# One kernel, one change: the weight panels of merge and output projection are split by ScalarE and VectorE instead of GpSimd

## The chip, the core and the metric

The kernel runs on one core of a Trainium2 chip. A core has five engines, each with its own queue of instructions, taken in order: TensorE (matrix products, into PSUM), VectorE and ScalarE (elementwise work, from and to SBUF and PSUM), GpSimd (elementwise work, SBUF only) and SyncE, which here issues all the DMA transfers. Engines wait for one another by semaphores. The metric is the time of one execution on the device, in microseconds.

In the profile's rows PE is TensorE (PEld its loads of stationary operands), DVE is VectorE, ACT is ScalarE, POOL is GpSimd and SP is SyncE; a q behind a name means the engine's sequencer.

## The reference, cut to what matters

One layer of a hybrid encoder is computed for two requests of 512 and 1024 tokens, 1536 tokens of 1024 channels in all. After the attention branch (`att`) and the state space branch (`y_ssm`) come:

```python
g = jax.nn.sigmoid(gates.reshape(b, S, 2, D_MODEL))
merged = g[:, :, 0] * (att @ w_proj_attn) + g[:, :, 1] * (y_ssm @ w_proj_ssm)
m = merged @ w_out
x = x + rmsnorm(m, norm_post_mix[l])
h = rmsnorm(x, norm_pre_ffn[l])
gate, up = jnp.split(h @ w_gate_up[l], 2, axis=-1)
f = (jax.nn.silu(gate) * up) @ w_down[l]
x = x + rmsnorm(f, norm_post_ffn[l])
```

All of it is float32. `w_proj_attn` and `w_out` are 1024 x 1024.

## The kernel before

**Products.** Every product is made of three: each operand `raw` is split into a high part `hi`, `raw` rounded to the matmul's reduced type, and a low part `lo = raw - hi`. `gemm` (L161) then adds hi x hi, hi x lo and lo x hi in PSUM, which are its lines L164, L165 and L166. So each weight panel costs a cast and a subtraction. `split` (L133) makes them, and its argument says on which engines: "act_dve" casts on ScalarE (L135) and subtracts on VectorE (L136), "act_pool" casts on ScalarE and subtracts on GpSimd (L138, L139), anything else does both on GpSimd (L141, L142).

**Panels.** `split_panel` (L144) loads a panel of 1024 x 256 weights in two halves of 128 partitions x 1024 elements, each of 512 KB, into tiles `wraw` (pool `rp`, two buffers), and splits each half into `whi` and `wlo` (pool `wp`, two buffers each, so two panels). By default it splits with "act_dve".

**The stages around the change.** The tokens go through the last part of the kernel in three chunks of 512. For chunk c:

- `load_att(c)` (L347): per head, loads a piece of attention and a broadcast row of scales (`araw`, three buffers), multiplies them (L353, VectorE), splits the product by "act_dve".
- `merge(c)` (L882): four panels of `w_proj_attn`, two blocks of 128 channels each. Per block: load `gt` (two buffers) and `pt` (one buffer), tanh of `gt` (L893, ScalarE), 24 matmuls of 512 columns, then L897 (VectorE, one input in PSUM), L898 (VectorE), L899 (ScalarE, high part of the result) and L900 (VectorE, its low part).
- `out_proj` (L1027): four panels of `w_out`, per panel four PSUM tiles of 24 matmuls of 256 columns each, each evicted by two ScalarE operations (L1035, L1037).
- `norms(c)` (L1040): two normalisations of the result. On VectorE L1053 and L1054 in eight pieces of 512 columns, each with a load of x (`xr`, two buffers) and a square on ScalarE (L1055), a chain of very small VectorE operations (`rsqrt`, L178 to L183), four L1061, then transposes on TensorE (L1065), evicted by ScalarE (L1067) and stored.

Chunk 0 has been merged during attention. The program writes, in this order: `out_proj` of chunk 0, `merge(1)`, `norms(0)`, `load_att(2)`, `out_proj` of chunk 1, `merge(2)`, `norms(1)`, the operands of the feed-forward's first product (`Operands`, `build`, VectorE and ScalarE), `out_proj` of chunk 2, first products, `norms(2)`.

**Order.** The order in which each engine takes its instructions is not the program's: a planner (`schedule_with_timeline_sim=True`) orders them by simulated times and its own costs, within the dependencies and the buffers. So work of one stage stands between that of another, and other engines for a piece of work can mean another order elsewhere. All loads and stores go through SyncE's one queue in the planned order: an issue that waits for a buffer holds those behind it.

Of the kernel before, what the change touches and what calls it, by code (L numbers as in the profile page):

```python
# [78 lines left out]
def hybrid_trunk_kernel(ctx: ExitStack, tc: tile.TileContext, a: dict, y_prompt, y_sample):  # L79
# [5 lines left out]
    def f(ap):  # L85
        return ap.bitcast(F32)
# [40 lines left out]
    def staged(pool, shape, *srcs, tag="raw", bufs=None):  # L127
        raw = pool.tile(shape, F32, tag=tag, name=tag, bufs=bufs)
        for part, src in srcs:
            load(out=raw[part] if part is not None else raw, in_=src)  # L130
        return raw

    def split(hi, lo, raw, eng=None):  # L133
        if eng == "act_dve":
            S.copy(hi, raw)  # L135
            V.tensor_sub(lo, raw, f(hi))  # L136
        elif eng == "act_pool":
            S.copy(hi, raw)  # L138
            G.tensor_sub(lo, raw, f(hi))  # L139
        else:  # L140
            G.tensor_scalar(hi, raw, 1.0, 0.0, op0=ALU.mult, op1=ALU.add)  # L141
            G.tensor_sub(lo, raw, f(hi))  # L142

    def split_panel(*srcs, eng="act_dve"):  # L144
        hi = wp.tile([P, KB, 256], F32R, tag="whi", name="whi")
        lo = wp.tile([P, KB, 256], F32R, tag="wlo", name="wlo")
        n = 256 // len(srcs)
        for s in (slice(0, 4), slice(4, 8)):
            raw = rp.tile([P, 4, 256], F32, tag="wraw", name="wraw")
            for i, src in enumerate(srcs):  # L150
                load(out=raw[:, :, i * n:(i + 1) * n], in_=src.rearrange("(a p) c -> p a c", p=P)[:, s])
            split(hi[:, s], lo[:, s], raw[:], eng)
        return hi, lo
# [20 lines left out]
        gemm(ps, [(act[0][:, k, ts_], act[1][:, k, ts_], hi[:, k, :], lo[:, k, :]) for k in range(KB)])  # L174

    def rsqrt(r, v, t):
        """r = v ** -0.5 for positive v: a first guess from the exponent, then Newton's steps"""
        V.tensor_scalar(r.bitcast(I32), v.bitcast(I32), 1, None, op0=ALU.logical_shift_right)  # L178
        V.tensor_scalar(r.bitcast(I32), r.bitcast(I32), -1.0, 1597463007.0, op0=ALU.mult, op1=ALU.add)
        for _ in range(3):  # L180
            V.tensor_mul(t, r, r)
            V.scalar_tensor_tensor(t, t, -0.5, v, op0=ALU.mult, op1=ALU.mult)
            V.scalar_tensor_tensor(r, t, 1.5, r, op0=ALU.add, op1=ALU.mult)  # L183
# [29 lines left out]
                next(others, None)  # L213

    def operands(base, SL, h, qk, qr, got):
        """the bias table, queries and keys of a head, in steps"""
        nkb = SL // P
        u0, un = P * (8 - nkb), SL + P * (nkb - 1)
        tb = qk.tile([P, un], F32, tag="tb", name="tb")
        load(out=tb, in_=sk_d[h, :, 127 + u0:127 + u0 + un])  # L220
        got["tb"] = tb
        halves = [slice(o, o + 512) for o in range(0, SL, 512)]
        for m in range(2):
            r = slice(h * P + m * 64, h * P + m * 64 + 64)
            q_h = qk.tile([P, SL], F32R, tag=f"qh{m}", name="qh")
            q_l = qk.tile([P, SL], F32R, tag=f"ql{m}", name="ql")
            q_r = staged(qr, [P, SL], *((slice(o, o + 64), q_d[r, base:base + SL]) for o in (0, 64)))
            S.copy(q_h[:], q_r[:])  # L228
            for s_ in halves:
                with behind():  # L230
                    G.tensor_sub(q_l[:, s_], q_r[:, s_], f(q_h[:, s_]))  # L231
                if QS: yield
            yield
            k_m = qk.tile([P, SL], F32R, tag=f"km{m}", name="km")
            k_r = staged(qr, [P, SL], *((slice(o, o + 64), k_d[r, base:base + SL]) for o in (0, 64)))
            S.copy(k_m[:], k_r)
            for s_ in halves:
                with behind():
                    G.tensor_sub(k_m[64:P, s_], k_r[64:P, s_], f(k_m[64:P, s_]))
                if QS: yield  # L240
            got[m] = (q_h, q_l, k_m)
            yield
# [3 lines left out]
    def behind():  # L246
        return tc.issue_after(last_add[-1].ins) if last_add and IA else nullcontext()
# [81 lines left out]
            pend.append(mean_square)  # L329

    def att_scale(g, zq, msq, pool, psp, ptag):
        """what the rows of attention are multiplied by: 1 / sum of exponentials and the norm"""
        n = zq.shape[-1]
        r, t = [pool.tile([P, 8, n], F32, tag=t_, name=t_, bufs=1) for t_ in ("att_r", "att_t")]
        V.reciprocal(t, zq)
        V.tensor_mul(zq, msq, t)
        V.tensor_mul(zq, zq, t)
        V.tensor_scalar(zq, zq, 1.0, EPS, op0=ALU.mult, op1=ALU.add)
        rsqrt(r[:], zq[:], msq[:])
        V.tensor_mul(r, r, t)  # L340
        ps = psp.tile([P, 512], F32, tag=ptag, name="rt")
        TE.transpose(ps[0:8 * n, 0:P], r[:].rearrange("p h j -> p (h j)"), ident)
        rt = pool.tile([P, P], F32, tag="att_rt", name="rt", bufs=1)
        V.tensor_copy(rt[0:8 * n], ps[0:8 * n, 0:P])
        store(out=r_d[g][:], in_=rt[0:8 * n])
# [10 lines left out]

    w_in = a["w_in"][0]

# [1 line left out]
    with ExitStack() as ph1:  # L360
        hp = ph1.enter_context(tc.tile_pool(name="hp", bufs=NCH, reuse_waits="tile"))
        st = ph1.enter_context(tc.tile_pool(name="st", bufs=2, reuse_waits="tile"))
# [4 lines left out]
        with tc.tile_pool(name="xa", bufs=2, reuse_waits="tile") as xa, tc.tile_pool(name="xa_ps", bufs=3, space=PSUM) as xps:  # L367
            natural_log_exp()
            for c in range(NCH):
# [19 lines left out]
                for j, xt in enumerate(tiles):  # L389
# [3 lines left out]
                    r = rsqrt_of(xa, ss, 1.0 / D, f"rs{j}")  # L393
# [49 lines left out]
        first = [split_panel(w_in[:, V0 + p0:V0 + p0 + 256], eng="pool") for p0 in (0, 256)]  # L443
# [57 lines left out]
        att_scale(0, zq, msq, pools[1], pools[5], "t")  # L501
        es.close()

        # step sizes and decays, for both directions at once
        sp = ph1.enter_context(tc.tile_pool(name="sp", bufs=1, reuse_waits="tile"))
        dts = sp.tile([P, NT, 32], F32, name="dts")
        tri = sp.tile([P, 2, P], F32, name="tri")
# [162 lines left out]
        for lo_c, hi_c in SEQS:  # L670
            state = [None, None]
# [40 lines left out]
        for lo_c, hi_c in SEQS:  # L712
            state = [None, None]
# [67 lines left out]

        gates(NG, 2 * D // P)

# [1 line left out]
    ap = ctx.enter_context(tc.tile_pool(name="ap", bufs=1, reuse_waits="tile"))  # L785
    zq, msq = [ap.tile([P, 8, 8], F32, name=n) for n in ("zq", "msq")]
    with ExitStack() as ph2:
# [3 lines left out]
        at = ph2.enter_context(tc.tile_pool(name="at", bufs=2, reuse_waits="tile"))  # L791
# [63 lines left out]
            pass  # L855
        pend.pop()()

# [1 line left out]
    with ExitStack() as ph3:  # L859
        big = ph3.enter_context(tc.tile_pool(name="big", bufs=7, reuse_waits="tile"))  # L860
        wk = ph3.enter_context(tc.tile_pool(name="wk", bufs=2, reuse_waits="tile"))
# [20 lines left out]
        def merge(c, aTt):  # L882
            cs = slice(c * 512, (c + 1) * 512)
            hi, lo = big_pair()
            for p0 in range(0, D, 256):
                w = split_panel(a["w_proj_attn"][0][:, p0:p0 + 256], eng="pool")
                for b in range(2):
                    r0 = p0 + b * P
                    kb = r0 // P
                    gt = wk.tile([P, 512], F32, tag="gt", name="gt")  # L890
                    pt = wk.tile([P, 512], F32, tag="pt", name="pt", bufs=1)
                    load(out=gt, in_=g_d[r0:r0 + P, cs])
                    S.activation(out=gt, in_=gt, func=AF.Tanh, scale=0.5)  # L893
                    load(out=pt, in_=part_d[r0:r0 + P, cs])
                    ps = mm_tile(512)
                    gemm_fm(ps, w, slice(b * P, (b + 1) * P), aTt)
                    V.scalar_tensor_tensor(gt, gt, 1.0, ps, op0=ALU.add, op1=ALU.mult)  # L897
                    V.tensor_add(gt, gt, pt)  # L898
                    S.activation(out=hi[:, kb, :], in_=gt, func=AF.Copy, scale=0.5)  # L899
                    V.scalar_tensor_tensor(lo[:, kb, :], gt, 0.5, f(hi[:, kb, :]), op0=ALU.mult, op1=ALU.subtract)  # L900
            return hi, lo

        # the feed-forward's first product by Strassen's scheme in Winograd's form: seven products of half size
        class Operands:
            names = ("b11", "t2", "t3", "t1", "b21", "t4", "b22")
            terms = {"b11": [(0, 0)], "t2": [(1, 1), (0, 1), (0, 0)], "t3": [(1, 1), (0, 1)], "t1": [(0, 1), (0, 0)],
# [115 lines left out]
        with ExitStack() as ph3a:  # L1022
# [4 lines left out]
            def out_proj(mT):  # L1027
                tiles = [mp.tile([P, D], F32, tag="mt", name="mt", bufs=4) for _ in range(4)]
                sums = wk.tile([P, 4, 4], F32, tag="ms4", name="ms4")
                for p0 in range(0, D, 256):  # L1030
                    w = split_panel(a["w_out"][0][:, p0:p0 + 256], eng="pool")
                    for j in range(4):
                        ps = mm_tile(256)
                        gemm_tm(ps, w, mT, slice(j * P, (j + 1) * P))
                        S.copy(tiles[j][:, p0:p0 + 256], ps)  # L1035
                        sq = wk.tile([P, 256], F32, tag="gt", name="msq")
                        S.activation(out=sq, in_=ps, func=AF.Square, accum_out=sums[:, j, p0 // 256:p0 // 256 + 1])  # L1037
                return tiles, sums
# [52 lines left out]
            w = {jb: weights(jb, "pt", 1) for jb in range(NPRE + NW)}  # L1091
# [17 lines left out]
    with ExitStack() as ph4:  # L1109
# [9 lines left out]
        for hf in range(2):  # L1119
# [11 lines left out]
            for t in range(NT):  # L1131
# [22 lines left out]
                r = rsqrt_of(yp, ss, 1.0 / D, "rs")  # L1154
# [44 lines left out]
```

## Time and profile before

| | us |
|---|---|
| three runs | 3272.72, 3287.25, 3288.95 |
| their median | 3287.25 |
| span of the profiled execution, first to last instruction | 3277.1 |

The profiled execution is one of its own; its time beside its span is not given apart, so only the span is known of it. It lies 10.2 us below the median of the runs.

A profile's page gives each engine's busy time, the span in 40 slices, the costliest groups of instructions by line, and the chain of work that ended last, followed back from the last instruction. Line numbers are the kernel's. In rows with arrows the tile that is written stands left of "<-". A helper's line, such as L142, stands for all its callers, and the tiles' names tell them apart.

### The profile page before, as it was taken

The page shows a single profiled execution, that of the slowest core. Times are in us where ns is not written, and L with a number is a line of the kernel's source. Part 1 is how long each engine was busy: PE and PEld are TensorE (multiplying, and loading weights), DVE is VectorE, ACT ScalarE, POOL GpSimd, SP SyncE. Part 2 cuts the span into 40 slices and gives each one's busy share as a digit, 9 for nine tenths or more (in the row PEclk, how much of TensorE's full clock was granted, in tenths as well). Part 3 has the DMA queues.
Part 4 walks back from the last instruction along what each step waited for, and adds up shares of the span by engine and source line. Part 5 has one row for each costly group of instructions (what it writes and reads, how often), then busy time and mean ns, then how long its engine had stood idle before and what let it go on. Part 6 is the DMA issues. An engine that isn't in the chain of part 4 may idle for free.

```text
span 3277.1 us, 44930 instructions
## 1 busy us (share of the span) xinstructions
PE 3068.7 (94%) x16688; PEld 2686.3 (82%) x16688; DVE 1887.9 (58%) x3048; ACT 1207.8 (37%) x2249; POOL 1086.4 (33%) x844
## 2 busy tenths in 40 slices
PE   7999999999899899999999888878999899989998
PEld 7988887889787677778888787677999899978787
DVE  5124444455238998277778765676656766642444
ACT  3013333233113333266666623243333333332343
POOL 1003332000244553167657544533333433310100
PEclk9999999999999999999999998888999999999999
DMA  4623332223553443655545146544333333363354
GB/s 145 193 97 114 112 100 76 67 74 108 174 164 124 130 133 118 200 168 172 178 144 182 39 139 221 172 132 154 98 97 106 96 100 99 110 202 94 117 166 131
DMA packets 442528, 430.00 MB, mean 131 GB/s; under 512 B 25324, under 2 KB 359617, under 8 KB 441245
## 3 DMA queue, kind: packets, MB, share of 16 engines
q1 hardware_dynamic: 442309, 427.12, 41.8%
q8 instruction: 132, 2.16, 0.3%
q14 instruction: 87, 0.71, 0.1%
HBM read 315.37 MB, written 120.05 MB: 133 GB/s over the span
## 4 chain that ended last, share of the span: by engine, by line
PE 57%; DVE 14%; DMA 12%; issue 8%; POOL 5%; ACT 4%; SPq 1%; POOLq 0%; DVEq 0%; ACTq 0%
PE acc L164 8%; PE acc L165 8%; PE acc L166 8%; PE mm L164 4%; PE mm L165 4%; PE mm L166 4%; PE d L166 3%; PE d L164 3%; PE d L165 3%; DMA wraw<-in_w_gate_up_dram 2%; DVE m L758 2%; DMA raw<-k_d 2%; DMA araw<-r_d 1%; PE s L290 1%; DVE m L752 1%
## 5 line engine op out<-in xcount | busy, mean ns | idle before, releaser
L164 PE MATMUL acc<-hT,whi 128*128 128x512 f32 (+1 forms) x1080 | 433.6, 402 | 5.8 <-ACT st L434 5.6
L165 PE MATMUL acc<-hT,whi 128*128 128x512 f32 (+1 forms) x1080 | 431.4, 399 | 0.0
L166 PE MATMUL acc<-hT,wlo 128*128 128x512 f32 (+1 forms) x696 | 273.8, 393 | 0.0
L164 PEld LDWEIGHTS acc<-hT,whi 128*128 128x128 f32 (+1 forms) x1080 | 203.6, 189 | 54.8 <-ACT st L434 6.6
L165 PEld LDWEIGHTS acc<-hT,whi 128*128 128x128 f32 (+1 forms) x1080 | 203.9, 189 | 45.6 <-issue 4.2
L296 ACT ACTIVATE pt<-pt,nm 128x1024 f32<-128x1024 f32 (+1 forms) x192 | 193.4, 1008 | 120.6 <-DVE nm L293 116.4
L293 DVE CUSTOM_DVE_ANT_0 pt<-s,tb 128x1024 f32<-128x1024 f32 (+1 forms) x192 | 197.6, 1041 | 64.5 <-PE s L291 51.2
L165 PE MATMUL acc<-wlo,hT 128*128 128x256 f32 x768 | 226.2, 295 | 0.0
L164 PE MATMUL acc<-whi,hT 128*128 128x256 f32 x768 | 224.6, 293 | 0.0
L166 PE MATMUL acc<-whi,hT 128*128 128x256 f32 x768 | 223.9, 292 | 0.0
L166 PE MATMUL d<-dhi,fl 128*128 128x512 f32 x528 | 207.6, 393 | 9.0 <-DVE fl L136 9.0
L164 PE MATMUL d<-dhi,fh 128*128 128x512 f32 x528 | 207.3, 393 | 8.1 <-DVE dlo L136 6.3
L165 PE MATMUL d<-dlo,fh 128*128 128x512 f32 x528 | 207.1, 392 | 0.0
L136 DVE TENSOR_TENSOR fl<-raw,fh 128x896 fp32r<-128x896 f32 (+1 forms) x72 | 85.9, 1195 | 199.7 <-ACT fh L135 199.7
L164 PE MATMUL mm<-op,wy 128*128 128x384 f32 x528 | 178.8, 339 | 10.2 <-ACT op L135 8.7
L166 PE MATMUL mm<-op,wy 128*128 128x384 f32 x528 | 178.7, 338 | 0.9 <-DVE wy L136 0.9
L165 PE MATMUL mm<-op,wy 128*128 128x384 f32 x528 | 178.3, 338 | 0.0
L302 POOL TENSOR_SCALAR pt<-pt,zs 128x512 f32<-128x512 f32 (+1 forms) x96 | 88.5, 921 | 253.9 <-DVE zs L300 212.6
L231 POOL TENSOR_TENSOR ql<-raw,qh 128x512 fp32r<-128x512 f32 x48 | 64.0, 1347 | 300.9 <-ACT qh L228 294.9
L166 PE MATMUL acc<-hT,whi 128*128 128x512 f32 x384 | 159.1, 414 | 0.0
L164 PEld LDWEIGHTS acc<-whi,hT 128*128 128x128 f32 x768 | 148.4, 193 | 8.9 <-issue 8.0
L135 ACT CAST whi<-wraw 128x1024 fp32r<-128x1024 f32 (+2 forms) x76 | 75.8, 1024 | 215.4 <-PE acc L166 99.6
(344 smaller groups left out, 8696.0 us busy)
## 6 DMA issues: line engine op xcount, KB each, us to landing
wraw<-in_w_in_dram SPq DMA_DIRECT2D x60, 512.0 KB
wraw<-in_w_gate_up_dram SPq DMA_DIRECT2D x92, 256.0 KB
raw<-ff_d SPq DMA_DIRECT2D x48, 448.0 KB
wr<-in_w_gate_up_dram SPq DMA_DIRECT2D x80, 256.0 KB
ff_d<-c SPq DMA_DIRECT2D x88, 192.0 KB
g_d<-st SPq DMA_DIRECT2D x48, 256.0 KB
xg<-xs_d SPq DMA_DIRECT2D x48, 256.0 KB
gt<-g_d SPq DMA_DIRECT2D x48, 256.0 KB
```

The costliest lines, as they stand in the source:

```text
L135: S.copy(hi, raw)
L136: V.tensor_sub(lo, raw, f(hi))
L164: TE.matmul(ps, ah, bh, start=(i == 0), stop=False)
L165: TE.matmul(ps, ah, bl, start=False, stop=False)
L166: TE.matmul(ps, al, bh, start=False, stop=(i == n - 1))
L231: G.tensor_sub(q_l[:, s_], q_r[:, s_], f(q_h[:, s_]))
L290: TE.matmul(sps[:, ks], qh[m][:, qs], km[m][:, ks], start=True, stop=False)
L293: V.tensor_tensor_reduce(out=pt[:], in0=sps[:], in1=tb[:, off:off + SL], scale=-1.0, scalar=3.0e38, op0=ALU.add, op1=ALU.min, accum_out=nm ...
L296: S.activation(out=pt, in_=pt, func=AF.Exp, bias=nm[:, m:m + 1], scale=-1.0, accum_out=(z0, zs[:, 0:1])[m])
L302: G.tensor_scalar(pm[1][:, cb], pm[1][:, cb], zs[:, 1:2], 0.0, op0=ALU.mult, op1=ALU.add)
L752: V.scalar_tensor_tensor(m, m, 1.0, cb[:, d_].unsqueeze(1).broadcast_to([P, 4, P]), op0=ALU.min, op1=ALU.mult)
L758: V.scalar_tensor_tensor(ms[0][:, h], ms[1][:, h], dts[:, c, 16 + hh + h:17 + hh + h], ms[0][:, h], op0=ALU.mult, op1=ALU.add)
```

## The change

`split_panel` is called in `merge` and in `out_proj` without the argument that put the splits on GpSimd, so that its default is used. GpSimd's cast and subtraction of each half become a cast on ScalarE and a subtraction on VectorE. The remaining edits of the diff take out comments and docstrings and leave the line numbers as they are.

```diff
@@ merge, L886 @@
-                w = split_panel(a["w_proj_attn"][0][:, p0:p0 + 256], eng="pool")
+                w = split_panel(a["w_proj_attn"][0][:, p0:p0 + 256])
@@ out_proj, L1031 @@
-                    w = split_panel(a["w_out"][0][:, p0:p0 + 256], eng="pool")
+                    w = split_panel(a["w_out"][0][:, p0:p0 + 256])
```

The helpers that it goes through are unchanged:

```python
    def split(hi, lo, raw, eng=None):
        if eng == "act_dve":
            S.copy(hi, raw)
            V.tensor_sub(lo, raw, f(hi))
        ...
        else:
            G.tensor_scalar(hi, raw, 1.0, 0.0, op0=ALU.mult, op1=ALU.add)
            G.tensor_sub(lo, raw, f(hi))

    def split_panel(*srcs, eng="act_dve"):
```

## Rows read from the trace of the kernel before

**Rows 1.** The head of the page: span and number of instructions, then each engine's busy time, its share of the span and its instructions.

```profile
span 3277.1 us, 44930 instructions
...
PE 3068.7 (94%) x16688; PEld 2686.3 (82%) x16688; DVE 1887.9 (58%) x3048; ACT 1207.8 (37%) x2249; POOL 1086.4 (33%) x844
```

**Rows 2.** The view of windows: start and end, length, then busy time and instructions of PE, PEld, DVE, ACT and POOL, the granted share of TensorE's clock, the DMA engines' mean busy share, and GB/s. Of the engines the first number is us.

```profile
1767.00:1800.00 33.00, 30.93 (x190) 26.33 (x189) 31.07 (x51) 20.75 (x36) 27.69 (x21) 1.00 0.69 230
1884.00:1932.00 48.00, 48.00 (x387) 48.00 (x388) 23.35 (x35) 14.38 (x46) 18.62 (x11) 0.96 0.43 132
1932.00:2012.00 80.00, 56.41 (x238) 45.09 (x237) 68.18 (x80) 21.13 (x50) 43.27 (x22) 0.86 0.61 202
2012.00:2058.00 46.00, 45.66 (x375) 45.41 (x374) 5.28 (x9) 17.58 (x58) 20.32 (x13) 0.98 0.56 181
2058.00:2136.00 78.00, 63.00 (x298) 51.86 (x297) 56.42 (x71) 20.36 (x43) 38.20 (x20) 0.89 0.54 182
2136.00:2174.00 38.00, 37.40 (x313) 37.20 (x310) 24.80 (x27) 16.07 (x52) 14.88 (x8) 1.00 0.47 146
```

**Rows 3.** The chain of work that ended last, from 1932 to 2012, by line: shares of this stretch.

```profile
by line: DVE mt L1053 12.1%; DVE araw L353 10.8%; DVE big L900 9.5%; issue 9.3%; DMA pt<-part_d 9.1%; DMA araw<-r_d 9.0%; DVE gt L898 8.1%; DVE mt L1054 7.0%; DMA xr<-in_x_prompt_dram 3.7%; DVE big L136 3.3%; DVE mv L1058 3.0%; ACT xr L1055
```

**Rows 4.** VectorE's groups from 1932 to 2012: line, engine, operation, written<-read tiles, shapes, count, then busy us and mean ns of one, then idle us before them and what ended it.

```profile
L900 DVE SCALAR_TENSOR_TENSOR big<-gt,big 128x512 fp32r<-128x512 f32 x6 | 10.6, 1773 | 0.8 <-ACT big L899 0.8
L1053 DVE SCALAR_TENSOR_TENSOR mt<-mt,mr,pmw 128x512 f32<-128x512 f32 x8 | 10.4, 1368 | 0.0
L353 DVE SCALAR_TENSOR_TENSOR araw<-araw,cols 128x512 f32<-128x512 f32 x8 | 10.3, 1283 | 9.6 <-DMA araw<-r_d 9.6
L1054 DVE TENSOR_TENSOR mt<-mt,xr 128x512 f32<-128x512 f32 x8 | 9.0, 1129 | 1.1 <-DMA xr<-in_x_prompt_dram 1.1
L898 DVE TENSOR_TENSOR gt<-gt,pt 128x512 f32<-128x512 f32 x6 | 8.2, 1372 | 0.4 <-DMA pt<-part_d 0.4
```

**Rows 5.** The same from 2058 to 2136.

```profile
L1053 DVE SCALAR_TENSOR_TENSOR mt<-mt,mr,pmw 128x512 f32<-128x512 f32 x8 | 11.3, 1478 | 0.1
L1054 DVE TENSOR_TENSOR mt<-mt,xr 128x512 f32<-128x512 f32 x8 | 8.5, 1073 | 4.4 <-DMA xr<-in_x_sample_dram 4.4
L900 DVE SCALAR_TENSOR_TENSOR big<-gt,big 128x512 fp32r<-128x512 f32 x8 | 7.5, 937 | 2.9 <-ACT big L899 2.8
L1061 DVE TENSOR_SCALAR mt<-mt,mr 128x1024 f32<-128x1024 f32 x4 | 6.9, 1781 | 0.0
L898 DVE TENSOR_TENSOR gt<-gt,pt 128x512 f32<-128x512 f32 x8 | 6.8, 854 | 1.9 <-DMA pt<-part_d 1.8
```

**Rows 6.** One line each over the whole span: line, engine, operation, tiles, count, then the shortest, median and longest duration in ns, first and last start in us, shapes.

```profile
L1053 DVE SCALAR_TENSOR_TENSOR mt<-mt,mr,pmw x24: 739/750/2884, 1946.4 to 2204.1; 128x512 f32<-128x512 f32 x24
...
L1054 DVE TENSOR_TENSOR mt<-mt,xr x24: 677/684/2252, 1956.7 to 2226.9; 128x512 f32<-128x512 f32 x24
...
L898 DVE TENSOR_TENSOR gt<-gt,pt x16: 679/688/2871, 1959.9 to 2125.4; 128x512 f32<-128x512 f32 x16
...
L900 DVE SCALAR_TENSOR_TENSOR big<-gt,big x16: 684/693/2885, 1963.6 to 2128.1; 128x512 fp32r<-128x512 f32 x16
...
L353 DVE SCALAR_TENSOR_TENSOR araw<-araw,cols x16: 741/752/2828, 1898.4 to 2019.4; 128x512 f32<-128x512 f32 x16
...
L897 DVE SCALAR_TENSOR_TENSOR gt<-gt,mm x16: 673/678/689, 1958.1 to 2124.6; 128x512 f32<-128x512 f32 x16
...
L1061 DVE TENSOR_SCALAR mt<-mt,mr x12: 741/749/2827, 1998.4 to 2237.9; 128x1024 f32<-128x1024 f32 x12
```

**Rows 7.** The timeline around 1950, instructions of a kind in a row merged: start us, us, engine, line, operation, tiles, shapes, count.

```profile
1948.40 8.38 DVE L1053 SCALAR_TENSOR_TENSOR mt<-mt,mr,pmw 128x512 f32<-128x512 f32 x5
...
1950.02 5.54 POOL L142 TENSOR_TENSOR wlo<-wraw,whi 128x1024 fp32r<-128x1024 f32 x2
```

**Rows 8.** GpSimd's splits by tile: its casts out of `wraw` between 1730 and 2240, and its subtractions into `wlo` between 1884 and 2180; columns as in rows 6.

```profile
L141 POOL TENSOR_SCALAR whi<-wraw x40: 1044/1050/1601, 1767.8 to 2155.7; 128x1024 fp32r<-128x1024 f32 x40
...
L142 POOL TENSOR_TENSOR wlo<-wraw,whi x36: 2342/2702/2857, 1900.5 to 2159.4; 128x1024 fp32r<-128x1024 f32 x36
```

**Rows 9.** Splits on ScalarE and VectorE elsewhere in the kernel, over the whole span; columns as in rows 6.

```profile
L135 ACT CAST whi<-wraw x76: 406/1050/1068, 92.3 to 2212.6; 128x1024 fp32r<-128x1024 f32 x72, 128x512 fp32r<-128x512 f32 x3, 128x256 fp32r<-128x256 f32 x1
...
L136 DVE TENSOR_TENSOR op<-rw,op x52: 539/551/2754, 2083.5 to 2575.2; 128x384 fp32r<-128x384 f32 x52
...
L136 DVE TENSOR_TENSOR wlo<-wraw,whi x41: 1025/1220/1254, 93.4 to 868.5; 128x1024 fp32r<-128x1024 f32 x40, 128x256 fp32r<-128x256 f32 x1
```

**Rows 10.** TensorE's waits for GpSimd, the first row from 1932 to 2012, the others from 2058 to 2136: who waited, for whom, us in total, times, longest us.

```profile
PE mm L166 <- POOL wlo L142: 10.2, 3, 7.1
...
PE mm L166 <- POOL wlo L142: 3.5, 2, 1.8
...
PE mm L164 <- POOL whi L141: 1.5, 1, 1.5
```

**Rows 11.** GpSimd's waits for loads and SyncE's for GpSimd, from 1884 to 2180; columns as in rows 10.

```profile
POOL whi L141 <- DMA wraw<-in_w_proj_attn_dram: 44.4, 10, 13.8
POOL whi L141 <- DMA wraw<-in_w_out_dram: 43.1, 10, 8.0
...
SPq L151 <- POOL wlo L142: 32.8, 10, 8.0
```

**Rows 12.** VectorE's largest group from 2136 to 2174; columns as in rows 4.

```profile
L136 DVE TENSOR_TENSOR op<-rw,op 128x384 fp32r<-128x384 f32 x14 | 12.7, 929 | 4.1 <-ACT op L135 4.0
```

## The prediction, made before the change was run

> **What bounds the kernel now.** I read the page first. Over the whole span TensorE is busy 94% of the time and GpSimd 33% [rows 1], which says that the kernel is bound by matmuls and that GpSimd's work is covered. That is an average over stages, so the next view is the windows, cut where the work around the change changes its kind [rows 2]. The reader is to see two kinds of stage there. Where `out_proj` runs alone (1884 to 1932, 2012 to 2058, 2136 to 2174) TensorE is busy from end to end: 48.00 of 48, 45.66 of 46, 37.40 of 38. There the splitting of the weight panels is hidden, on whichever engine. Where `merge` runs together with `norms` (1932 to 2012 and 2058 to 2136, called the first and the second merge stage below) TensorE is busy 56.41 of 80 and 63.00 of 78 at a granted clock of 0.86 and 0.89, while VectorE is busy 68.18 of 80 and 56.42 of 78. What the change is worth is decided in these two.
>
> The third view is the chain of the first merge stage [rows 3]: VectorE's lines L1053, L353, L900, L898 and L1054 lead it, with loads (`pt`, `araw`) between them. TensorE does not set the end there.
>
> The fourth view says why VectorE is so busy. Its groups in the two stages [rows 4, 5] have means of 1.07 to 1.77 us for operations that elsewhere take 0.68 to 0.75 us: the shortest L1053 is 739 ns and the longest 2884, L898 is 679 and 2871, L900 684 and 2885 [rows 6]. L897, in the same stages and of the same size, takes 673 to 689 ns and never more [rows 6]; it reads one input from PSUM, the drawn-out ones (L1061 too, 741 and 2827) read from SBUF alone. The long ones coincide with GpSimd's subtractions: from 1950.02 GpSimd has two `wlo` in 5.54 us, and five L1053 from 1948.40 need 8.38 us instead of the 3.7 that five times 739 ns make [rows 7]. One GpSimd `wlo` lasts 2342 to 2857 ns [rows 8], the length of a long VectorE operation. So I read it thus: a VectorE operation that reads from SBUF alone and meets a GpSimd subtraction stands until that one has ended.
>
> **The change part by part.** It removes GpSimd's splits of `merge` and `out_proj`: 40 casts (median 1.05 us) and 40 subtractions (2.70 us) [rows 8]. In their place come 40 ScalarE casts of 128x1024 (median 1.05 us) and 40 VectorE subtractions of the same shape (1.22 us) [rows 9]. Loads, matmuls and tiles stay. 36 of the 40 halves stand after 1884, the first subtraction at 1900.5 and the last at 2159.4; the other four from 1767.8 on, in the end of attention [rows 8].
>
> *First merge stage, what goes.* VectorE's excess over the shortest time, for the five largest groups [rows 4, 6]: L900 6 x (1.773 - 0.684) = 6.5, L1053 8 x (1.368 - 0.739) = 5.0, L353 8 x (1.283 - 0.741) = 4.3, L1054 8 x (1.129 - 0.677) = 3.6, L898 6 x (1.372 - 0.679) = 4.2. Together 23.6 us. No other GpSimd work stands in this stage, so all of it should go.
>
> *What comes.* Some 10 of the 36 halves fall into this stage: the four panels of `merge` and the first of the next `out_proj`, two halves each (by share of the time, 36 x 80 / 262 = 11). On VectorE 10 x 1.22 = 12.2 us, on ScalarE 10 x 1.05 = 10.5 us; ScalarE is busy 21.13 of 80 [rows 2] and has the room. Net on VectorE: 23.6 - 12.2 = 11.4 us less, and VectorE is on the chain.
>
> *The holds.* TensorE waits 10.2 us for `wlo` in this stage [rows 10]. GpSimd needs 3.75 us for a half (1.05 + 2.70) where cast and subtraction on two engines need 2.27 in sequence. Behind it the load queue waits too: SyncE stands 32.8 us between 1884 and 2180 for `wlo` to free a `wraw` buffer [rows 11], and the loads of `gt`, `pt` and `xr` stand behind the panel's load. These holds run beside VectorE's chain, so I count half of the 10.2 us, about 5. First stage: 11.4 + 5 = 16 us. It can't exceed 80 - 56.4 = 23.6 us at the present clock, and it is nothing where loads set the pace.
>
> *Second merge stage.* The same sum [rows 5, 6]: L1053 8 x (1.478 - 0.739) = 5.9, L1054 8 x (1.073 - 0.677) = 3.2, L900 8 x (0.937 - 0.684) = 2.0, L898 8 x (0.854 - 0.679) = 1.4, L1061 4 x (1.781 - 0.741) = 4.2: 16.7 us. Against it 8 halves, 9.8 us. Net 6.9. TensorE waits 3.5 + 1.5 = 5.0 us for GpSimd [rows 10]; here the last panel waits, whose results the next product needs, so I count it whole. Together 12 us, of at most 78 - 63 = 15.
>
> *Last `out_proj` (2136 to 2174).* VectorE builds operands of the next product there: 14 x (0.929 - 0.551) = 5.3 us of excess over the median [rows 9, 12], against 4 halves, 4.9 us. TensorE is full. Nothing, with 5 us either way for the stage behind it.
>
> *End of attention.* Four halves add 4.9 us to a VectorE that is busy 31.07 of 33, and take 4 x 3.75 = 15 us from a GpSimd that is busy 27.69 of 33 [rows 2, 8]. TensorE is busy 30.93 there. I take nothing, and 5 us either way.
>
> *What is queued behind.* ScalarE and VectorE take their instructions in order. A cast now waits for its panel's load, and behind it stand L893, L899 and L1055; the subtraction waits for the cast, and behind it L897, L898 and L1054. GpSimd's casts waited 44.4 us for the loads of `w_proj_attn` and 43.1 us for those of `w_out` [rows 11], with nothing behind them. I take these waits at nothing more than now, since each half's buffer is freed 2.27 us after its load has landed, where GpSimd casts both halves before it subtracts [rows 7]; the other end is the second rival. A planner writes the order of all queues anew, by its own costs; where it puts the casts the trace of before can't show, and the same rival and the range hold it.
>
> The sum: 16 + 12 = 28 us. The profiled execution's span is 3277.1 us, so it would be 3249; that span stands 10.2 us below the median of the runs, and what lies around it is not known. Against the median: 3287.25 - 28 = 3259 us.
>
> [...]
>
> **The rivals.** *The loads set the pace.* `pt` (one buffer) and `araw` stand in the chain [rows 3], the stage moves 202 GB/s [rows 2], and a VectorE that is ready sooner waits for the same loads. For it: VectorE is idle in the second stage for 22 of 78 us already. Against it: the loads' issue waits for VectorE and GpSimd in turn [rows 11]. Then only TensorE's 5.0 us for GpSimd in the second stage go: 3282 us. [...]
>
> *The waits move onto ScalarE and VectorE*, the case on the other side. Of the 87.5 us that GpSimd waits for loads, each one left standing in ScalarE's order holds the evictions behind it. It decides from 28 / 87.5, a third, on the chain: 3287 us. At a half: 3287 + 44 - 28 = 3303 us. For it: `wraw` has two buffers, so a panel's load can't be issued much ahead. Against it: the freeing is sooner.
>
> *TensorE's floor.* Both stages shrink to TensorE's own work: 23.6 + 15, the clock back at full for some 14% of 56 and 11% of 63, about 8 + 7: 53 us. 3234 us. For it: all of GpSimd's holds go at once. Against it: the loads.
>
> That the change does nothing can't be: each split names its engines.
>
> **How the numbers follow.** The forecast has 0.50 (its own range 3242 to 3271), the loads 0.20, the moved waits 0.17, the floor 0.13. The range goes from the floor, 3232, to the middle of the moved waits' 3287 to 3303 and a little more, 3296; outside are some 0.04 below and 0.12 above. Half a percent, 16 us, is about what a measurement of this kernel can tell from no change (the three runs of before differ by as much). Faster by over that: the floor, nearly all of the forecast and a little of the loads, 0.64. Within it: most of the loads, a little of the forecast and two fifths of the moved waits, 0.26. Slower: the rest of these, 0.10.
>
> **What would show it.** Right: L1053, L898, L900 and L1054 at 0.68 to 0.75 us throughout; the two merge stages about 64 and 66 us long; no wait of TensorE for `wlo` over 2 us; SyncE's wait for `wlo` well under 32.8 us. Wrong: ScalarE's casts of `whi` waiting tens of us for the panels' loads; the stages no shorter though VectorE's operations are; or VectorE's operations still long, and then GpSimd was not the cause.

## The result, and the profile after

The changed kernel takes 3249.32 us (median of four runs, 3243.93 to 3255.13), the kernel before 3285.62 us (four runs, 3272.72 to 3288.95): a ratio of 0.9896 with a 95% interval of 0.9874 to 0.9918. A second set of runs gave 0.9897 (0.9872 to 0.9922). By the ratio some 34 us are gained (36 between the two medians); 28 were forecast. Against the median that made 3259 us, in a range of 3232 to 3296, and 3249 lies in it. That it equals the 3249 which the prediction reckoned from the profiled span is chance.

The head of the page after shows GpSimd and VectorE busy for less time, ScalarE for more, and TensorE's share unchanged [rows 1]:

```profile
span 3253.4 us, 44920 instructions
...
PE 3066.6 (94%) x16688; PEld 2689.0 (83%) x16688; DVE 1868.7 (57%) x3088; ACT 1249.1 (38%) x2289; POOL 939.3 (29%) x764
```

VectorE has 40 instructions more and is busy 19.2 us less. The two spans differ by only 23.7 us, less than the runs do, because the two executions differ already before the first changed instruction (1767.8 [rows 8]): the last of twelve subtractions into `yTt`, a line untouched by the change, starts at 1687.4 us in before's trace and at 1699.2 in after's. Spans of single executions are therefore not compared below. What is compared is one stretch, called *the stage*: from the first matmul of chunk 0's output product to the first matmul of the feed-forward's first product. It holds both merge stages and all three output products. The view of windows, first before, then after (columns as in rows 2):

```profile
1884.00:2175.70 291.70, 250.46 (x1602) 227.56 (x1602) 179.44 (x223) 91.21 (x251) 135.28 (x72) 0.92 0.53 174
```

```profile
1899.90:2155.40 255.50, 243.25 (x1603) 224.84 (x1604) 151.10 (x260) 128.98 (x295) 0.00 (x0) 0.96 0.60 197
```

The stage is 36.2 us shorter (in the second trace of the changed kernel it is 252.1 us long). TensorE's idle time falls from 291.7 - 250.5 = 41.2 us to 12.3, and its busy time by 7.2 us at a granted clock of 0.96 instead of 0.92. VectorE took over 36 subtractions, 36 x 1.22 = 43.9 us, and is busy 28.3 us *less*. The stage cut as rows 2 cut it:

```profile
1900.00:1949.00 49.00, 49.00 (x388) 48.80 (x387) 23.72 (x41) 20.71 (x54) 0.00 (x0) 0.94 0.43 130
1949.00:2029.00 80.00, 69.18 (x368) 59.05 (x366) 58.19 (x101) 41.52 (x79) 0.00 (x0) 0.95 0.74 255
2029.00:2061.00 32.00, 31.23 (x241) 31.23 (x242) 4.72 (x4) 13.35 (x43) 0.00 (x0) 0.90 0.38 123
2061.00:2125.00 64.00, 63.33 (x357) 55.26 (x356) 45.53 (x83) 32.55 (x55) 0.00 (x0) 1.00 0.69 226
2125.00:2155.00 30.00, 30.00 (x252) 30.00 (x251) 18.57 (x33) 20.35 (x66) 0.00 (x0) 1.00 0.54 172
```

In the first merge stage (second row) TensorE still stands for 11 of 80 us, but it does 368 matmuls there where it did 238: the merge's own matmuls, from the first to the last, take 48.4 us instead of 59.0, so more of the output product behind them falls into the 80 us. In the second (fourth row) it is busy 63.33 of 64 at a clock of 1.00, against 63.00 of 78 at 0.89.

VectorE's operations are short again; one line each over the whole span (columns as in rows 6):

```profile
L898 DVE TENSOR_TENSOR gt<-gt,pt x16: 681/688/693, 1962.8 to 2118.3; 128x512 f32<-128x512 f32 x16
...
L900 DVE SCALAR_TENSOR_TENSOR big<-gt,big x16: 681/684/693, 1968.9 to 2120.2; 128x512 fp32r<-128x512 f32 x16
...
L1054 DVE TENSOR_TENSOR mt<-mt,xr x24: 674/685/1787, 1969.5 to 2204.2; 128x512 f32<-128x512 f32 x24
...
L353 DVE SCALAR_TENSOR_TENSOR araw<-araw,cols x16: 744/751/752, 1915.0 to 2013.7; 128x512 f32<-128x512 f32 x16
...
L1053 DVE SCALAR_TENSOR_TENSOR mt<-mt,mr,pmw x24: 743/746/1779, 1963.6 to 2182.9; 128x512 f32<-128x512 f32 x24
...
L1061 DVE TENSOR_SCALAR mt<-mt,mr x12: 744/749/754, 2005.2 to 2217.6; 128x1024 f32<-128x1024 f32 x12
```

L900 reached 2885 ns before and now no more than 693. The long values left, L1053's 1779 and L1054's 1787, are of `norms(2)`, behind the stage, where GpSimd works for the feed-forward.

What TensorE waits for from the first merge stage to the stage's end (columns as in rows 10), after:

```profile
PE mm L164 <- ACT msq L1037: 3.7, 1, 3.7
PE mm L166 <- DVE big L900: 2.6, 2, 2.3
PE mm L166 <- DVE wlo L136: 2.5, 2, 2.1
PE tr_ps L1065 <- ACT hr L1067: 2.2, 2, 1.6
```

and before:

```profile
PE tr_ps L1065 <- DVE mt L1061: 14.0, 5, 8.4
PE mm L166 <- POOL wlo L142: 13.7, 5, 7.1
PE mm L164 <- ACT big L899: 5.5, 4, 2.6
PE mm L166 <- DVE big L900: 3.5, 2, 2.4
```

Two waits are gone: 13.7 us for `wlo`, which the change was aimed at, and 14.0 us at the transposes (`tr_ps`) for L1061, VectorE's last step of `norms`, which the prediction hadn't priced.

### The profile page after: what moved, and what is told of

Same layout as the page of the kernel before. It is cut to its first block, busy times and chain, and to the rows that moved or that the text cites. A ratio compares the mean times of both kernels' runs of the same rounds, so it can differ in the third digit from the quotient of the medians.

```text
span 3253.4 us, 44920 instructions
## 1 busy us (share of the span) xinstructions
PE 3066.6 (94%) x16688; PEld 2689.0 (83%) x16688; DVE 1868.7 (57%) x3088; ACT 1249.1 (38%) x2289; POOL 939.3 (29%) x764
## 5 line engine op out<-in xcount | busy, mean ns | idle before, releaser
L135 ACT CAST whi<-wraw 128x1024 fp32r<-128x1024 f32 (+2 forms) x116 | 116.2, 1031 | 226.4 <-PE acc L166 100.0
L136 DVE TENSOR_TENSOR fl<-raw,fh 128x896 fp32r<-128x896 f32 (+1 forms) x72 | 85.9, 1195 | 199.2 <-ACT fh L135 191.1
L136 DVE TENSOR_TENSOR wlo<-wraw,whi 128x1024 fp32r<-128x1024 f32 (+1 forms) x81 | 96.2, 1217 | 115.6 <-ACT whi L135 106.3
L135 ACT CAST fh<-raw 128x896 fp32r<-128x896 f32 (+1 forms) x72 | 70.8, 983 | 227.7 <-PE d L165 213.5
```

## The experiments

Two theories. *Stalls*: VectorE's operations stand behind GpSimd's, and taking GpSimd away gives VectorE time back. *Holds*: the panels were ready late because GpSimd is slow (2.70 us for a subtraction [rows 8] that takes VectorE 1.22 [rows 9]), and TensorE waited for them. VectorE's *stalls* below are the sum, over its operations in the stage, of what each takes above the tenth percentile of its line, tiles and shape: 70.4 us before, 1.5 after. Ratios are to the kernel before, on the same chip, with 95% intervals.

| kernel | ratio | stage, us | VectorE busy in it | its stalls | TensorE waits for GpSimd | at transposes for L1061 |
|---|---|---|---|---|---|---|
| before | 1 | 291.8 | 179.5 | 70.4 | 15.8 | 14.0 |
| after | 0.9896 (0.9874 to 0.9918) | 255.4 | 151.1 | 1.5 | 0 | 0 |
| again | 0.9897 (0.9872 to 0.9922) | 252.1 | 151.0 | 1.6 | 0 | 0 |
| e2 | 1.0037 (1.0018 to 1.0056) | 292.4 | 206.0 | 61.1 | 0 | 2.9 |
| e8 | 0.9973 (0.9961 to 0.9986) | 278.5 | 180.1 | 31.2 | 0 | 3.9 |
| e7 | 0.9947 (0.9930 to 0.9964) | 266.8 | 168.7 | 22.6 | 0 | 3.2 |
| e12 | 0.9955 (0.9937 to 0.9972) | 272.4 | 186.3 | 1.6 | 0 | 0.5 |
| e5 | 1.0003 (0.9987 to 1.0020) | 296.9 | 177.3 | 66.3 | 2.1 | 39.0 |
| e1 | 0.9948 (0.9927 to 0.9969) | 271.2 | 151.5 | 41.4 | 8.9 | 14.8 |
| e10 | 0.9916 (0.9893 to 0.9939) | 267.7 | 150.3 | 39.5 | 4.5 | 13.7 |
| e3 | 0.9914 (0.9890 to 0.9938) | 260.8 | 161.4 | 35.2 | 0 | 2.9 |
| e4 | 0.9979 (0.9963 to 0.9995) | 273.4 | 167.7 | 36.1 | 16.8 | 2.3 |
| e9 | 0.9886 (0.9868 to 0.9905) | 254.7 | 152.2 | 7.1 | 0 | 0 |
| e11 | 0.9882 (0.9856 to 0.9908) | 253.8 | 151.8 | 6.9 | 0 | 0 |

**e2: GpSimd busy again, with work that nobody waits for.** To the changed kernel, one GpSimd subtraction per half panel is added, 32 in all (every panel but chunk 0's `out_proj`); it reads `whi`, and nothing reads what it writes.

```diff
+jt = wy.tile([P, 4, 256], F32, tag="wy6"); V.memset(jt, 0.0)
 split(hi[:, s], lo[:, s], raw[:], eng)
+G.tensor_sub(jt, jt, f(hi[:, s]))
```

> The changed kernel, and beside each panel half from the first merge on (32 of the 40) one more GpSimd subtraction of 128x1024 out of whi into a tile that nobody reads. Nothing waits for it but the later reuse of whi, and the planned order of all other engines is the changed kernel's. Theory A (the gain is VectorE no longer standing behind GpSimd's subtractions): VectorE's L1053, L1054, L898, L900 are drawn out again to up to 2.9 us, and most of the gain is lost: 3272 to 3285 us. Theory B (the gain is that a panel is ready sooner, so TensorE and the load queue wait less): the panels are ready as soon as in the changed kernel, so within 5 us of its 3249.

Measured: 1.0037. The whole gain is gone, and a little more. The order of every engine's other instructions is that of the changed kernel, ScalarE's casts into `whi` never waited for the added reads, and ScalarE's operations are no longer than there, so another order or a panel held by the added reads isn't the cause. One line each in e2:

```profile
L900 DVE SCALAR_TENSOR_TENSOR big<-gt,big x16: 677/688/2901, 1970.2 to 2149.9; 128x512 fp32r<-128x512 f32 x16
```

```profile
L152 POOL TENSOR_TENSOR jt<-jt,whi x32: 2377/2875/3485, 1938.7 to 2170.4; 128x1024 f32<-128x1024 f32 x32
```

```profile
L897 DVE SCALAR_TENSOR_TENSOR gt<-gt,mm x16: 673/676/689, 1959.1 to 2142.2; 128x512 f32<-128x512 f32 x16
```

L900 is back at up to 2901 ns, the length of the added subtraction, and L897, with one input from PSUM, stays at 689. TensorE waits for what VectorE and ScalarE make instead: 15.0 us for `big` (L899) and 11.7 for `wlo` (L136). That GpSimd's subtractions, merely by running, cost this stage tens of microseconds through VectorE is shown: 32 of them make it 38.6 us longer than the mean of the two traces of the changed kernel, 253.8 us.

**e8 and e7: less of it.** e8 adds the same subtraction to `merge`'s 16 halves only. e7 replaces it by a cast with one input, on all 32:

```diff
-G.tensor_sub(jt, jt, f(hi[:, s]))
+G.tensor_scalar(jt, f(hi[:, s]), 1.0, 0.0, op0=ALU.mult, op1=ALU.add)
```

> The changed kernel with the extra GpSimd subtractions beside merge's panels alone (16 instead of 32). If all stalls of VectorE weigh alike, half of the 40 us lost with 32 of them: about 3269 us. If, as the two halves of the change say (GpSimd on out_proj's panels cost nothing, on merge's two thirds of the gain), only those beside merge count: 3280 to 3288 us.

> The changed kernel with 32 extra GpSimd operations that have one input (the cast of 128x1024, 1.05 us) in place of the subtractions with two (2.4 us). If VectorE stands for as long as GpSimd works: 1.05 / 2.4 of the 40 us, so 3263 to 3270 us, with VectorE operations drawn out by up to 1 us. If only GpSimd's two-input operations hold it: 3246 to 3255 us and no VectorE operation drawn out.

Measured: e8 0.9973, about half of e2's loss for half of its subtractions (by the stage 24.7 of 38.6 us). e7 0.9947: casts stall VectorE too: beside casts of 1048 to 2050 ns L900 took up to 1527 ns, with a median of 688; one line each, of e7:

```profile
L152 POOL TENSOR_SCALAR jt<-whi x32: 1048/1410/2050, 1942.8 to 2147.5; 128x1024 f32<-128x1024 f32 x32
```

```profile
L900 DVE SCALAR_TENSOR_TENSOR big<-gt,big x16: 678/688/1527, 1968.1 to 2128.7; 128x512 fp32r<-128x512 f32 x16
```

So before's 40 casts were part of the disturbance (in its trace the L1054 that started at 1956.70 met a cast alone and took 1522 ns, against 684 at the median), which the prediction had put down to the subtractions.

**e12: the same extra work on VectorE itself,** `V.tensor_sub(jt, jt, f(hi[:, s]))` in e2's place, 32 times 1.22 us.

> The changed kernel with the 32 extra subtractions on VectorE itself (32 x 1.22 = 39 us more work there, none on GpSimd). With the extra GpSimd subtractions VectorE's busy time rose by 55 us (61 us of stalls) and the stage by 37, so 0.67 us for each. If a microsecond of VectorE costs this whatever it is spent on: 0.67 x 39 = 26 us, 3270 to 3277 us. If it is where the stalls fall (in the chain of norms and in the splits themselves, unforeseen by the planner) that makes them dear, plain work that the planner knows of fits into VectorE's idle 100 us: 3246 to 3258.

Measured: 0.9955, 3266.57 us, between the two ranges. It prices VectorE's time without such stalls (1.6 us of them, against 61.1 in e2), but in an order that the planner made for it, where e2, e7 and e8 keep the changed kernel's. Against the mean stage of the two traces of the changed kernel (253.8 us, VectorE 151.1): (272.4 - 253.8) / (186.3 - 151.1) = 0.53 us of stage per microsecond of VectorE. The kernels with stalls come out higher by the same reckoning: e2 38.6 / 54.9 = 0.70, e7 13.0 / 17.6 = 0.74, e8 24.7 / 29.0 = 0.85. Before has 28.4 us more VectorE time than after; at 0.53 to 0.85 that is 15 to 24 of its 38 us. These are averages over the whole stage; the next section looks at the two stretches of it that the transposes wait for.

**e5: the holds alone.** The kernel before, where every second panel from the first `merge` on is loaded into two tiles that are idle then, so that four `wraw` stand in place of two:

```diff
-raw = rp.tile([P, 4, 256], F32, tag="wraw", name="wraw")
+raw = wy.tile([P, 4, 256], F32, tag=f"wy{4 + s.start // 4}", name="wraw") if odd else rp.tile(...)
```

> The kernel before, with four buffers for the raw halves from the first merge on (every second panel takes two buffers that the feed-forward uses later), GpSimd's work and the planned order otherwise nearly unchanged. Theory A (contention): nothing that holds VectorE changes, within 5 us of the kernel before. Theory B (holds: a panel is late since its load waits for GpSimd to free the raw buffer): TensorE's waits for wlo and SyncE's 32.8 us for it shrink: 8 to 16 us faster than before.

Measured: 1.0003. The holds did go, and nothing came of it. TensorE's waits in e5's stage:

```profile
PE tr_ps L1065 <- DVE mt L1061: 39.0, 5, 23.1
PE mm L164 <- ACT big L899: 5.6, 4, 2.6
PE mm L164 <- ACT whi L135: 3.8, 1, 3.8
PE mm L166 <- POOL wlo L142: 2.1, 1, 2.1
```

For GpSimd it waits 2.1 us instead of 15.8, at the transposes 39.0 instead of 14.0. The two merges' own matmuls take 47.7 and 43.7 us where they took 59.0 and 49.6, as short as in the changed kernel (48.4 and 43.7), and all of it is lost again behind them. The holds lay beside VectorE's chain: with VectorE as late as before, TensorE only stands somewhere else.

**e1: only the casts moved.** In both calls `eng="act_pool"`: casts on ScalarE, subtractions left on GpSimd.

> Only the casts move to ScalarE; GpSimd keeps the 40 subtractions. A: the subtractions are what holds VectorE, so its excess of some 50 us in the two merge stages stays by and large: 3278 to 3288 us. B: a half is ready after 1.05 + 2.7 us still, but GpSimd has 2.7 us of work a half instead of 3.75, so about a third of the gain: 3270 to 3277 us.

Measured: 0.9948, a larger gain than either theory's range allowed. VectorE's stalls fall from 70.4 to 41.4 us with the casts, and the stage by 20.6, 0.71 us for each, as in e2. But VectorE is then as busy as in after (151.5 us; 41.4 us of stalls there stand against 43.9 us of subtractions here), and the stage is still 17.4 us longer. Its waits of TensorE:

```profile
PE tr_ps L1065 <- DVE mt L1061: 14.8, 3, 7.3
PE mm L166 <- POOL wlo L139: 8.9, 5, 2.2
```

**e10: e1 with e5's buffers,** to see whether the holds count once VectorE is relieved.

> The casts on ScalarE, the subtractions on GpSimd, and four buffers for the raw halves. New theory C: two things bound the merge stages side by side, VectorE's time (with its stalls) and the moment at which GpSimd has a panel ready; taking one away shows only as far as the other allows. With the casts alone gone VectorE was busy for 151.5 us from the first output product to the feed-forward, as in the changed kernel (151.1), and the stage still took 271 us against 255. By C the buffers, which were worth nothing in the kernel before, are worth something here: TensorE's 8.9 us of waits for GpSimd shrink and the time falls by 6 to 14 us below the version with the casts alone (3257): 3243 to 3251 us. If the buffers never matter: 3254 to 3260.

Measured: 0.9916, 3251.43 us, at the edge of what the holds would give. The waits for GpSimd fall from 8.9 to 4.5 us and the stage by 3.5, but those at the transposes stay at 13.7, and the intervals of e1 and e10 overlap. So the 17 us aren't settled by it. The waits at the transposes, 13.7 to 14.8 us in before, e1 and e10, are at most 3.9 in every other kernel but e5, that is, in each where VectorE has some of these splits. In some of these the planner also puts the transposes later in TensorE's queue: in after 68 matmuls of the next output product stand between the first merge and the first transpose, and 14 behind the second merge; in before none and none, in e1 9 and none. The order alone isn't the cause, for e4, with 2.3 us of waits there, has 15 and none, much like e10 (12 and none).

What the rows add is that VectorE itself is later in e1. From the first matmul of the first merge to the last L1061 of the norms beside it e1 takes 67.9 us and after 60.0; VectorE is busy 48.8 us of it in e1 and 49.8 in after, but in e1 it stands longer for a load, first e1, then after:

```profile
DVE araw L353 <- DMA araw<-r_d: 13.9, 4, 7.1
```

```profile
DVE araw L353 <- DMA araw<-r_d: 5.2, 2, 5.0
```

Beside the second merge it is 52.8 us against 47.3. Why VectorE gets its loads later in e1, and whether the order or the panels' earlier readiness saves the 17 us, was not separated and stays open.

**e3 and e4: one call at a time.** e3 is the changed kernel with `out_proj`'s panels back on GpSimd, e4 with `merge`'s.

> The panels of merge by ScalarE and VectorE, those of out_proj by GpSimd as before. A: about half of the GpSimd subtractions that fall into the merge stages are out_proj's first panels and stay: 3260 to 3272 us. B: before, all waits of TensorE for GpSimd stood at merge's matmuls, so nearly the whole gain: 3249 to 3256 us.

> The panels of out_proj by ScalarE and VectorE, those of merge by GpSimd as before. A: the other half of the gain: 3262 to 3274 us. B: TensorE's waits for merge's panels stay: 3278 to 3288 us.

Measured: e3 0.9914, 3248.96 us, the lower end of theory B's range; e4 0.9979, 3272.73 us, within the range of A. `merge`'s panels alone carry nearly the whole gain, though both leave about the same stalls (35.2 and 36.1 us). What differs in the rows is the holds. In e4:

```profile
PE mm L164 <- POOL whi L141: 9.3, 2, 7.9
PE mm L166 <- POOL wlo L142: 7.5, 4, 3.0
```

These 16.8 us are 0 in e3, and the two merges' own matmuls take 59.4 and 49.0 us in e4, 48.3 and 43.7 in e3. That `merge` needs its panels while it leads, and `out_proj` has time for its own, is a reading of these rows; no run tests it alone.

**e9 and e11: chunk 0's output product left on GpSimd.** Its splits stand where TensorE is full from end to end and partly in the end of attention.

```diff
-t0 = out_proj(m0)
+t0 = out_proj(m0, "pool")
```

> The changed kernel, but the panels of chunk 0's out_proj stay on GpSimd. Their first two are split at the end of attention, which was 3 to 4 us shorter in all profiles where GpSimd made them; the merge stages keep the whole gain. 3243 to 3249 us, so some 3 us better than the changed kernel; if that difference was the planner's order elsewhere, 3249 to 3254.

> The changed kernel with chunk 0's out_proj on GpSimd and four buffers for the raw halves after it. TensorE is busy for 241 of the 255 us of the stage and waits nowhere for a load of a panel, so by C the buffers give nothing more: within 4 us of the version without them (3243). A gain of 5 or more would say that loads of panels still held ScalarE's or VectorE's queue.

> The changed kernel once more, beside the others on one chip: 0.987 to 0.992 of the kernel before, and in the profile about 255 us from the first output product to the feed-forward. If the version with chunk 0 on GpSimd is truly better, this one is 3 to 4 us longer, at the end of attention.

Measured: 0.9886 for e9 and 0.9882 with e5's buffers added (e11), against 0.9896 and 0.9897 for the change itself: the lowest of all, but not clear of it by the intervals. What is steady is the end of attention, from the last L812 to the stage's first matmul: 101.9 to 104.1 us in the seven kernels that split chunk 0's panels with GpSimd's help (before, e1, e3, e5, e9, e10, e11), 106 to 110 in the others (after 106.9 and 106.4).

## Why the prediction was right, step by step

- **VectorE stands behind GpSimd** (rows 6 and 7): right, and shown by e2 (L900 up to 2901 ns there, up to 693 in after). **The excess was counted too small.** Only the largest groups were in it: 23.6 us in the first merge stage, 16.7 + 5.3 behind it. All VectorE operations of the stage together lost 70.4 us, 30.0 of it between the two merges' first matmuls and 34.9 from the second's to the stage's end. The many small operations and the splits of operands belong to it. (The means in rows 4 and 5 go from 0.85 to 1.78 us, not from 1.07 to 1.77.)
- **The net on VectorE, 11.4 + 6.9 us, counted one for one as time:** about right where it was meant. The transposes wait for what VectorE does from a merge's first matmul to the last L1061 of the norms beside it. These two stretches before, then after (columns as in rows 2):

```profile
1931.85:2002.34 70.49, 51.29 (x209) 40.38 (x207) 58.52 (x75) 18.26 (x45) 35.69 (x19) 0.86 0.63 208
2057.74:2114.30 56.56, 45.98 (x197) 36.18 (x195) 45.77 (x61) 12.60 (x30) 30.56 (x16) 0.96 0.48 163
```

```profile
1948.61:2008.57 59.96, 56.06 (x276) 46.95 (x275) 49.76 (x90) 30.30 (x58) 0.00 (x0) 0.97 0.82 284
2060.99:2108.28 47.29, 47.23 (x224) 39.46 (x222) 37.30 (x73) 23.35 (x42) 0.00 (x0) 1.00 0.72 234
```

VectorE is busy 8.8 and 8.5 us less, and the stretches are 10.5 and 9.3 us shorter, 1.15 us for each; in the second TensorE is now busy from end to end. By the same reckoning against after e2's two stretches come to 35.8 / 39.5 = 0.91 and e12's to 27.8 / 34.9 = 0.80. Over the whole stage VectorE's net is 28.4 us, and the price 0.53 to 0.85.
- **What the second merge stage's sum left out** stands behind its last L1061: from there to the stage's end 61.4 us became 47.1, which is 14.3 us. Before, then after:

```profile
2114.30:2175.70 61.40, 54.68 (x413) 53.10 (x413) 36.85 (x40) 25.59 (x69) 22.52 (x12) 0.90 0.54 175
```

```profile
2108.30:2155.40 47.10, 46.49 (x390) 46.19 (x389) 27.14 (x43) 29.93 (x80) 0.00 (x0) 1.00 0.57 182
```

TensorE has fewer matmuls left there, waits less, and its granted clock is 1.00 where it was 0.90. The last `out_proj` has no part in it, as forecast: the stage's last 309 matmuls take 39.7 us before and 40.2 after.
- **The holds, 5 + 5 us, as a term of their own:** wrong as argued. e5 took 13.7 us of them away and gained nothing. They count, if at all, only once VectorE is relieved (e1 to after, 17.4 us), and there the share of the holds and that of the planner's order are open. These 10 us stand in the sum in place of the 14.3 that it left out, so that the total came out so near is in part luck.
- **First merge stage 16, second 12 us.** From the first matmul of the first merge to that of the second, 125.9 us became 112.4 (109.5 in the second trace): 13.5 to 16.4, as forecast. From there to the stage's end 118.0 became 94.4 (94.1), where TensorE is busy 93.7: 24, twice the forecast. Here the floor was reached, with the clock back at 1.00; that was the third rival's case, in one of the two stages.
- **The stages' lengths of 64 and 66 us** were a poor sign to name: other matmuls fall between the cuts, so the windows don't hold the same work. TensorE's longest wait for `wlo` is 2.1 us, where none over 2 was to be seen.
- **End of attention, 0 with 5 either way:** a loss of 2.3 to 2.8 us against the trace of before.
- **"Behind it the load queue waits too":** this sign failed. SyncE's wait for `wlo`, to refill `wraw`, was to be well under 32.8 us and is as long as before [rows 11]:

```profile
SPq L151 <- DVE wlo L136: 32.9, 23, 7.8
```

It did no harm that the rows show: the casts wait little for their loads (next line). That the queue merely runs ahead of its two buffers is likely, not tested.
- **The moved waits, the rival on the slower side,** didn't come: ScalarE's casts of `w_proj_attn`'s panels wait little for their loads, where GpSimd's waited 44.4 us [rows 11]:

```profile
ACT whi L135 <- DMA wraw<-in_w_proj_attn_dram: 5.2, 4, 2.1
```

With so short a wait most of these loads must have landed when ScalarE came to their casts. The loads didn't set the pace either: the first merge stage moves 255 GB/s where it moved 202 [rows 2].

## What to carry to other kernels

In these runs GpSimd's work wasn't free where VectorE leads, even when nobody waited for its result: 32 such subtractions made the stage 38.6 us longer (e2). Moving 40 casts from GpSimd to ScalarE and 40 subtractions from GpSimd, busy 33%, to VectorE, busy 58%, made VectorE itself less busy (1868.7 us where it was 1887.9). Look for it by comparing the shortest and the longest of a line in the view by line, sum the excess over *all* operations of the stage, and price a microsecond of the engine that leads by adding some harmless work to it. Such a price is an average over the stage: in the two stretches that ended with what TensorE waited for it was 0.80 to 1.15 here. Removing a wait by buffers alone shows whether it was a bound or lay beside another one.

## What the runs showed of the hardware

VectorE operations that read only SBUF lasted up to about as long as the GpSimd operations that they met: L900 up to 2901 ns beside subtractions (e2), up to 1527 beside casts of 1048 to 2050 (e7), at most 693 without (after). In before's trace a subtraction runs from 1963.10 to 1965.95 us, and the L900 that starts inside it, at 1963.61, ends at 1966.49, after 2885 ns. GpSimd's operations are not of one length either: the 32 equal subtractions of e2 took 2377 to 3485 ns.

L897, with one of its inputs from PSUM, took 673 to 689 ns in the traces of before, after, e2 and e7; in that of before four of its sixteen ran from start to end beside a GpSimd operation and took 673 to 681. L1061 reads one large tile (and `mr`, a small one), both from SBUF, and is drawn out as well: beside two subtractions, from 2107.41 us on, two in a row took 2815 and 2827 ns, where it takes 749 at the median [rows 6]; in after none took over 754. By what means GpSimd's operation holds up VectorE's, and why L897 is spared, no run here shows.
